# A kernel that plans its own order of work gets other prices for its instructions

## The chip, the cores and the metric

The kernel runs on one core of one Trainium2 chip. The metric is the device time of one execution in microseconds (us). The core has five instruction queues that work in order and wait for each other by semaphores: TensorE (PE, with its weight loads as PEld), VectorE (DVE), ScalarE (ACT), GpSimd (POOL) and SyncE (SP), which issues every DMA here.

## The reference

The program is a two-layer backbone over 1024 latent tokens and, in the first layer, 256 context tokens, 1024 channels wide, in float32. What a layer computes:

```
h = modulate(rms_norm(x, norm1_g[l]), sh1, sc1)        # sh, sc, g from a conditioning vector
p = h @ w_in[l]                                        # columns of four head groups
y_a = fourier_mix(p[..., 0:256])                       # 2-D FFT, real part
y_b = neighbourhood_attention(q, k, v, k_ctx, v_ctx, rpb, rows)     # 8x16 windows, and the context
y_c = spatial_gating(p[..., 1024:1536], ...)           # gelu, layer norm, matmul over chunks of 128
y_d = diff_post(diff_latent(q, k, v, ...))             # (softmax(s1) - lam * softmax(s2)) @ v, rope
x = x + g1 * (concat(y_a, y_b, y_c, y_d) @ w_out[l])
h2 = modulate(rms_norm(x, norm2_g[l]), sh2, sc2)
x = x + g2 * (square(relu(h2 @ w_ff1[l])) @ w_ff2[l])
```

The context tokens go the same way in the first layer; a final RMSNorm ends it.

## The kernel before, in words

Channels lie on the 128 partitions and tokens along the free axis, in blocks of 512, 512 and 256 (BLK). To keep precision, each float32 operand is split into a high and a low part that TensorE takes in its fast format (F32R), and a product is three matmuls (`mm3`, L394). ACT makes the high part, DVE or POOL subtracts it to get the low one (`split`, L358).

By time, layer 0 has its projections and attention until about 900 us and its MLP until about 1700; layer 1 has projections and attention until about 2400, then a last MLP in seven products in place of eight (`mlp_last`, L1488), and the final norm.

The text of the kernel doesn't fix the order of the instructions. Every call of an engine goes to the class `Plan`, whose `add` (L131) records it with the earlier instructions that it depends on, the tiles that it uses, a rank and a price (`cost`, L160). At the end `flush` (L186) plays a list schedule: of the five engines it takes the one that can start first (L250 to L261); among the instructions of that engine that are ready by then it takes the one of lowest rank, then the first recorded (L262 to L265); it lets the engine be busy for the price, and lets those that depend on it become ready at the end of it plus `LAT`, 0.13 us (L274; from matmul to matmul without it). A DMA keeps SP for 0.06 us, the transfers follow one another at 320 KB a us, and data lands a fixed latency later (L267 to L270). Tiles have few buffers, so an instruction can also wait for the release of one. The order found is then issued as it is (L286), and each engine keeps to it. That is why nearly every instruction in the profile has the line L286; tiles are told apart by name.

The ranks come from `run(rank, erank, ...)` (L576): `rank` is for PE, `erank` for the other engines. In a layer, differential attention has rank 1 (L1952). Behind it on PE, at rank 2, stand Fourier, gating and the projections of neighbourhood attention (L1951), whose other engines have 0.5, ahead of attention; then neighbourhood attention at 3 (L1953), then the first part of the output projection at 4 (L1957). They fill PE's time while attention isn't ready.

A unit of differential attention (`unit`, L1040) writes scores (tile ds) into three PSUM banks, takes the maximum with DVE (mx, nm), the exponential with its sum with ACT (e), joins the two softmaxes on DVE, or on DVE and POOL. Then PE transposes (tp), ACT and DVE split the result (pt), and PE multiplies it with the values (pvd). Neighbourhood attention does the same with nsl and nsc, npt and pvn.

Other names: dks and dqs are keys and queries reloaded, wh, wl and w weights, nvw the values of neighbourhood attention written in 16 windows at a time (`put_nv`, L947), fr the squared relu of the first MLP, fy, fyh and fyl the Fourier result, its high and its low part.

Of the kernel before, what the change touches and what calls it, by code (L numbers as in the profile page):

```python
# [11 lines left out]
F32R = mybir.dt.float32r  # L12
# [4 lines left out]
PSUM = bass.MemoryType.PSUM  # L17
# [16 lines left out]
class Plan:  # L34
# [8 lines left out]
    def __init__(self, tc):  # L43
        self.tc, self.nc = tc, tc.nc
        self.rank = self.erank = 0.0
        self.ops = []
        self.done = 0
        self.hist = {}
        self.tiles = {}
        self.tags = {}  # L50
        self.masks = {}
        self.free = {}
        self.idle = []
        self.dma_free = 0.0


    def pool(self, pool):
# [102 lines left out]
    def cost(self, eng, method, outs, ins, kw):  # L160
        def width(a):
            n = 1
            for _, k in a.ap[1:]:
                n *= k
            return n

        n = max(width(a) for a in outs + ins)
        if eng == "tensor":
            n = width(outs[0])
            c = 1 if ins[0].dtype == F32R else 2 if method == "transpose" else 4  # L170
            return max(n, 128 if c == 4 else 64) * c / 2400.0
        if eng == "sync":
            b = 4
            for _, k in outs[0].ap:
                b *= k
            return b
        if eng == "scalar":
            return 0.093 + n / 1200.0 + (0.13 if kw.get("accum_out") is not None else 0.0)
        if eng == "vector":
            ptr = any(isinstance(kw.get(k), bass.AP) for k in ("scalar", "scalar1", "scalar2"))  # L180
            fast = method in ("tensor_scalar", "tensor_copy", "memset") and all(a.space != PSUM for a in outs + ins)
            return 0.065 + 0.065 * ptr + n / (1920.0 if fast else 960.0)
        return 0.1 + n / 470.0


    def flush(self):  # L186
        ops, base = self.ops, self.done
        n = len(ops)
        left, succ, ready = {}, {}, {}
        tiles, tags = self.tiles, self.tags  # L190
        waiting = {}
        engines = ("tensor", "vector", "scalar", "gpsimd", "sync")
        future = {e: [] for e in engines}
        avail = {e: [] for e in engines}

        def allocate(key):
            q = tags[key]
            while q[2] < q[0] and q[1]:
                t = q[1].pop(0)
                q[2] += 1  # L200
                tiles[t][2] = q[3]
                for i in waiting.pop(t, ()):
                    settle(i, q[3])

        def settle(i, t):
            ready[i] = max(ready[i], t)
            left[i] -= 1
            if left[i] == 0:
                heapq.heappush(future[ops[i][0]], (ready[i], i))

        pend = {}
        for i in range(base, n):
            for t in ops[i][5]:
                pend[t] = pend.get(t, 0) + 1

        def release(t):
            q = tags[tiles[t][0]]
            if q[1]:
                q[2] -= 1
                q[3] = max(q[3], tiles[t][3])  # L220
                allocate(tiles[t][0])
            else:
                self.idle.append(t)

        idle, self.idle = self.idle, []
        for t in idle:
            if t not in pend:
                release(t)
        for key in tags:
            allocate(key)  # L230
        for i in range(base, n):
            o = ops[i]
            left[i] = 1
            ready[i] = 0.0
            for j in o[4]:
                if j >= base:
                    left[i] += 1
                    succ.setdefault(j, []).append(i)
                else:
                    ready[i] = max(ready[i], ops[j][8])  # L240
            for t in o[5]:
                if tiles[t][2] is None:
                    left[i] += 1
                    waiting.setdefault(t, []).append(i)
                else:
                    ready[i] = max(ready[i], tiles[t][2])
            settle(i, 0.0)
        order = []
        while len(order) < n - base:
            best = None  # L250
            for e in engines:
                f = self.free.get(e, 0.0)
                if avail[e]:
                    s = f
                elif future[e]:
                    s = max(f, future[e][0][0])
                else:
                    continue
                if best is None or s < best[0]:
                    best = (s, e)  # L260
            s, e = best  # L261
            while future[e] and future[e][0][0] <= s:  # L262
                _, i = heapq.heappop(future[e])
                heapq.heappush(avail[e], (ops[i][6], i))
            _, i = heapq.heappop(avail[e])  # L265
            o = ops[i]
            if e == "sync":  # L267
                self.free[e] = s + 0.06
                self.dma_free = max(self.dma_free, s) + max(0.3, o[7] / 320e3)
                end = self.dma_free + 1.9  # L270
            else:
                end = s + o[7]
                self.free[e] = end
            o[8] = end + self.LAT  # L274
            order.append(i)
            for k in succ.get(i, ()):
                settle(k, end if e == "tensor" and ops[k][0] == "tensor" else o[8])
            for t in o[5]:
                pend[t] -= 1
                tl = tiles[t]  # L280
                tl[3] = max(tl[3], o[8])
                if pend[t] == 0:
                    release(t)
        for i in order:
            o = ops[i]
            ins = o[1](*o[2], **o[3])  # L286
            self.tc.keep_in_program_order(ins)
            o[1] = o[2] = o[3] = None
        self.done = n
# [1863 lines left out]
```

## Time and profile before

| what | us |
|---|---|
| median of 3 runs (lowest, highest) | 3067.13 (3064.72, 3068.18) |
| the profiled execution, its own time | 3063.9 |
| its span, first to last instruction | 3062.1 |
| PE busy | 2860.1 |
| DVE busy | 2036.7 |
| ACT busy | 1370.6 |
| POOL busy | 735.9 |
| mean granted clock of PE | 0.972 |

The busy time of an engine is the time in which at least one of its instructions ran. Instructions of one engine can overlap at their ends, so the spacing of two starts can be shorter than a duration. A wait in the profile is idle time of an engine just before an instruction, put down to whatever ended it.

### The profile page before, as it was taken

The page shows a single profiled execution, that of the slowest core. Times are in us where ns is not written, and L with a number is a line of the kernel's source. Part 1 is how long each engine was busy: PE and PEld are TensorE (multiplying, and loading weights), DVE is VectorE, ACT ScalarE, POOL GpSimd, SP SyncE. Part 2 cuts the span into 40 slices and gives each one's busy share as a digit, 9 for nine tenths or more (in the row PEclk, how much of TensorE's full clock was granted, in tenths as well). Part 3 has the DMA queues.
Part 4 walks back from the last instruction along what each step waited for, and adds up shares of the span by engine and source line. Part 5 has one row for each costly group of instructions (what it writes and reads, how often), then busy time and mean ns, then how long its engine had stood idle before and what let it go on. Part 6 is the DMA issues. An engine that isn't in the chain of part 4 may idle for free. (4 is left out here: it accounts for less than half of the span.)

```text
span 3062.1 us, 42936 instructions
## 1 busy us (share of the span) xinstructions
PE 2860.1 (93%) x14994; PEld 2352.7 (77%) x14994; DVE 2036.7 (67%) x3753; ACT 1370.6 (45%) x2974; POOL 735.9 (24%) x507
## 2 busy tenths in 40 slices
PE   6898999999999999999999888898998999999997
PEld 3776787776788888888888777777786778878876
DVE  7477886586866677665333647786785875576765
ACT  5466555475423233222122436655564544454332
POOL 5235222243522122112112303311110022122200
PEclk8898999999999999999999999999999999999998
DMA  6644345677347886674211364445688664464465
GB/s 229 193 131 135 104 125 154 238 248 254 97 138 246 285 277 216 221 239 137 65 39 45 131 194 128 148 155 167 215 281 305 226 211 145 145 219 149 150 228 177
DMA packets 291632, 550.60 MB, mean 180 GB/s; under 512 B 35924, under 2 KB 84692, under 8 KB 288344
## 3 DMA queue, kind: packets, MB, share of 16 engines
q1 hardware_dynamic: 291416, 547.86, 54.4%
q8 instruction: 118, 1.93, 0.3%
q14 instruction: 98, 0.80, 0.1%
HBM read 388.58 MB, written 162.88 MB: 180 GB/s over the span
## 5 line engine op out<-in xcount | busy, mean ns | idle before, releaser
L286 POOL TENSOR_TENSOR wl<-wr,wh 128x512 fp32r<-128x512 f32 (+2 forms) x260 | 360.5, 1408 | 919.8 <-ACT wh L286 894.6
L286 PE MATMUL sx<-bq,sh 128*128 128x512 f32 x2304 | 548.4, 396 | 10.3 <-ACT q L286 3.2
L286 PEld LDWEIGHTS sx<-bq,sh 128*128 128x128 f32 x2304 | 431.1, 188 | 121.3 <-DVE bq L286 6.5
L286 DVE TENSOR_REDUCE mx<-ds 128x1 f32<-128x512 f32 (+1 forms) x320 | 218.4, 686 | 131.8 <-PE ds L286 129.9
L286 ACT ACTIVATE e<-ds,nm 128x512 f32<-128x512 f32 (+1 forms) x400 | 241.3, 611 | 121.2 <-DVE nm L286 111.3
L286 ACT ACTIVATE wh<-wr 128x512 fp32r<-128x512 f32 (+2 forms) x260 | 152.5, 614 | 316.9 <-issue 139.4
L286 PE MATMUL f<-hidh,wh 128*128 128x512 f32 (+1 forms) x768 | 278.1, 362 | 6.9 <-ACT hh L286 4.1
L286 PE MATMUL f<-hidl,wh 128*128 128x512 f32 (+1 forms) x768 | 277.0, 361 | 0.0
L286 PE MATMUL f<-hidh,wl 128*128 128x512 f32 (+1 forms) x768 | 277.0, 361 | 0.0
L286 PE MATMUL f<-hh,wh 128*128 128x512 f32 (+1 forms) x768 | 274.5, 357 | 0.0
L286 PE MATMUL f<-hh,wl 128*128 128x512 f32 (+1 forms) x768 | 274.2, 357 | 0.0
L286 PE MATMUL f<-hl,wh 128*128 128x512 f32 (+1 forms) x768 | 274.2, 357 | 0.0
L286 PE MATMUL pj<-hh,wh 128*128 128x512 f32 (+1 forms) x512 | 194.8, 381 | 21.2 <-DMA wh<-wd 9.4
L286 DVE SCALAR_TENSOR_TENSOR x<-f,ada,x 128x512 f32<-128x512 f32 (+1 forms) x192 | 125.5, 658 | 130.8 <-PE f L286 130.5
L286 PE MATMUL pj<-hl,wh 128*128 128x512 f32 (+1 forms) x512 | 193.4, 378 | 2.3 <-POOL hl L286 1.9
L286 PE MATMUL pj<-hh,wl 128*128 128x512 f32 (+1 forms) x512 | 193.0, 377 | 0.5 <-DMA wl<-wd 0.5
L286 ACT ACTIVATE sh<-wq 128x512 fp32r<-128x512 f32 x160 | 99.2, 628 | 202.0 <-DMA wd<-sh 49.1
L286 POOL TENSOR_TENSOR e<-e 128x1280 f32<-128x1280 f32 (+1 forms) x36 | 98.4, 2733 | 378.5 <-DVE e L286 239.1
L286 POOL TENSOR_TENSOR ws<-wq 128x512 f32<-128x512 f32 x54 | 76.8, 1422 | 416.6 <-DVE sh L286 233.6
L286 DVE TENSOR_TENSOR fr<-fr 128x512 f32<-128x512 f32 (+1 forms) x96 | 84.7, 882 | 133.7 <-ACT fr L286 133.5
L286 PE MATMUL ds<-dks,dqs 128*128 128x512 f32 (+1 forms) x400 | 143.0, 393 | 32.2 <-ACT e L286 18.8
L286 PEld LDWEIGHTS f<-hidh,wh 128*128 128x128 f32 x768 | 146.5, 191 | 31.1 <-ACT hh L286 4.5
(315 smaller groups left out, 6577.4 us busy)
## 6 DMA issues: line engine op xcount, KB each, us to landing
wd<-sh SPq DMA_DIRECT2D x99, 512.0 KB, 3.9
wr<-in_w_ff SPq DMA_DIRECT2D x144, 256.0 KB, 3.1
ar<-in_ada_w SPq DMA_DIRECT2D x112, 256.0 KB, 3.7
bq<-hid SPq DMA_DIRECT2D x24, 1024.0 KB, 6.8
wq<-in_w_ff1s SPq DMA_DIRECT2D x76, 256.0 KB, 3.1
sh<-wd SPq DMA_DIRECT2D x66, 256.0 KB, 4.2
wq<-in_w_ff2s SPq DMA_DIRECT2D x64, 256.0 KB, 4.2
wr<-in_ada_w SPq DMA_DIRECT2D x48, 256.0 KB, 3.8
```

Of the source, the lines that this page charges most:

```text
L286: ins = o[1](*o[2], **o[3])
```

## The change: other prices in the planner, and a port that two engines share

`cost` gets other formulas for every engine: durations with a fixed part and a part by elements, those of ACT depending on whether an operand is in PSUM. A new function `shares` tells which instructions use the SBUF port that DVE and POOL have in common: all of POOL, and of DVE those with two inputs in SBUF, and copies and scalar operations on SBUF. In `flush` such an instruction starts no earlier than the end of the last one that used the port. The latency of a DMA behind its transfer becomes 2.6 us. Ranks, `LAT`, SP's 0.06 us and the instructions themselves stay.

```diff
--- before.py
+++ after.py
@@ -52,6 +52,7 @@
         self.free = {}
         self.idle = []
         self.dma_free = 0.0
+        self.port = 0.0
 
 
     def pool(self, pool):
@@ -167,20 +168,35 @@
         n = max(width(a) for a in outs + ins)
         if eng == "tensor":
             n = width(outs[0])
-            c = 1 if ins[0].dtype == F32R else 2 if method == "transpose" else 4
-            return max(n, 128 if c == 4 else 64) * c / 2400.0
+            if ins[0].dtype == F32R:
+                return max(0.112, 0.006 + n / 2265.0)
+            if method == "transpose":
+                return 0.107
+            return max(0.224, n / 600.0)
         if eng == "sync":
             b = 4
             for _, k in outs[0].ap:
                 b *= k
             return b
+        near = any(a.space == PSUM for a in ins)
         if eng == "scalar":
-            return 0.093 + n / 1200.0 + (0.13 if kw.get("accum_out") is not None else 0.0)
+            return (0.165 if near else 0.195) + n / 1200.0 + (0.21 if kw.get("accum_out") is not None else 0.0)
         if eng == "vector":
             ptr = any(isinstance(kw.get(k), bass.AP) for k in ("scalar", "scalar1", "scalar2"))
             fast = method in ("tensor_scalar", "tensor_copy", "memset") and all(a.space != PSUM for a in outs + ins)
-            return 0.065 + 0.065 * ptr + n / (1920.0 if fast else 960.0)
-        return 0.1 + n / 470.0
+            return 0.15 + 0.06 * ptr + n / (1920.0 if fast else 960.0)
+        return 0.2 + n / 465.0
+
+    def shares(self, o):
+
+        if o[0] == "gpsimd":
+            return True
+        if o[0] != "vector":
+            return False
+        ins = [v for k, v in o[3].items() if k in ("in_", "in0", "in1") and isinstance(v, bass.AP)]
+        if any(a.space == PSUM for a in ins):
+            return False
+        return len(ins) > 1 or o[9] in ("tensor_scalar", "tensor_copy")
 
 
     def flush(self):
@@ -267,8 +283,11 @@
             if e == "sync":
                 self.free[e] = s + 0.06
                 self.dma_free = max(self.dma_free, s) + max(0.3, o[7] / 320e3)
-                end = self.dma_free + 1.9
+                end = self.dma_free + 2.6
             else:
+                if self.shares(o):
+                    s = max(s, self.port)
+                    self.port = s + o[7]
                 end = s + o[7]
                 self.free[e] = end
             o[8] = end + self.LAT
```

## Rows read from the trace of the kernel before

**Rows 1.** Busy line of the page: engine, busy us, share of the span, instructions.

```profile
PE 2860.1 (93%) x14994; PEld 2352.7 (77%) x14994; DVE 2036.7 (67%) x3753; ACT 1370.6 (45%) x2974; POOL 735.9 (24%) x507
```

**Rows 2.** Table by stage: stretch, us, busy us of PE, PEld, DVE, ACT, POOL; clock; DMA.

```profile
0.00:100.00 100.00, 66.84 (x277) 46.16 (x278) 72.93 (x131) 53.32 (x89) 48.22 (x36) 0.85 0.65 226
100.00:900.00 800.00, 736.53 (x4252) 596.92 (x4251) 561.15 (x1238) 438.65 (x1114) 268.72 (x196) 0.97 0.52 162
900.00:1700.00 800.00, 798.25 (x4155) 676.96 (x4154) 452.44 (x636) 210.49 (x381) 162.10 (x114) 1.00 0.53 176
1700.00:2500.00 800.00, 718.61 (x4005) 600.09 (x4004) 584.14 (x1240) 424.00 (x1022) 157.90 (x90) 0.96 0.62 200
2500.00:3000.00 500.00, 496.01 (x2118) 396.73 (x2118) 330.18 (x440) 231.15 (x350) 91.49 (x66) 1.00 0.51 176
3000.00:3062.00 62.00, 43.85 (x195) 35.84 (x193) 35.90 (x69) 12.98 (x20) 7.44 (x6) 0.83 0.47 160
```

**Rows 3.** Waits of PE: tile, what ended them, us in total, times, longest us.

```profile
PE ds L286 <- ACT e L286: 18.8, 25, 2.7
...
PE ds L286 <- DMA dks<-dk: 9.7, 3, 4.8
PE pj L286 <- DMA wh<-wd: 9.4, 2, 6.9
...
PE wo L286 <- DMA w<-wd: 5.9, 6, 3.6
...
PE tp L286 <- DVE e L286: 4.9, 6, 1.5
...
PE pvn L286 <- DVE npt L286: 3.1, 7, 0.7
...
PE pvd L286 <- DVE pt L286: 2.6, 8, 0.6
```

**Rows 4.** DVE in groups of one shape: out<-in, count, busy us, mean ns, idle before.

```profile
L286 DVE TENSOR_REDUCE mx<-ds 128x1 f32<-128x512 f32 x256 | 175.3, 687 | 131.1 <-PE ds L286 129.4
...
L286 DVE TENSOR_TENSOR pt<-tp,pt 128x512 fp32r<-128x512 f32 x168 | 111.4, 684 | 30.1 <-ACT pt L286 28.9
...
L286 DVE SCALAR_TENSOR_TENSOR e<-e,dr 128x1280 f32<-128x1280 f32 x32 | 52.8, 1650 | 0.6
...
L286 DVE TENSOR_TENSOR fr<-fr 128x256 f32<-128x256 f32 x32 | 40.5, 1265 | 17.8 <-ACT fr L286 17.8
...
L286 DVE TENSOR_SCALAR e<-e,dr 128x1280 f32<-128x1280 f32 x32 | 29.4, 918 | 0.9
```

**Rows 5.** Timeline of 1951 to 1963 us: start, us, instruction, idle before and its end.

```profile
1951.48 0.16 DVE L286 TENSOR_REDUCE nm<-mx 128x1 f32<-128x3 f32 x1
...
1951.67 0.69 ACT L286 ACTIVATE e<-ds,nm 128x512 f32<-128x512 f32 x1 [0.53 <-DVE nm L286]
...
1952.35 0.68 ACT L286 ACTIVATE e<-ds,nm 128x512 f32<-128x512 f32 x1
...
1955.23 0.68 DVE L286 TENSOR_TENSOR fy<-fT,fT 128x512 f32<-128x512 f32 x1
...
1955.94 0.63 ACT L286 ACTIVATE fyh<-fy 128x512 fp32r<-128x512 f32 x1 [2.36 <-DVE fy L286]
...
1960.31 1.28 DVE L286 TENSOR_TENSOR pt<-tp,pt 128x512 fp32r<-128x512 f32 x2
```

**Rows 6.** Timeline of 2088 to 2102 us, SP's queue and then PE.

```profile
2088.18 7.59 SPq L286 DMA_DIRECT2D nvw<-vt  x16
...
2101.86 0.80 PE L286 MATMUL pj<-hh,wh 128*128 128x512 f32 x1 [6.93 <-DMA wh<-wd]
```

**Rows 7.** Table as rows 2, of a stretch after a wait and one without idle.

```profile
2095.00:2107.00 12.00, 5.14 (x15) 4.09 (x16) 1.71 (x5) 2.25 (x7) 1.71 (x1) 0.57 0.78 238
...
2500.00:2600.00 100.00, 100.00 (x430) 80.55 (x430) 61.65 (x92) 50.30 (x82) 20.86 (x16) 1.00 0.46 156
```

**Rows 8.** DMA issues: count, KB each, median us from issue to landing.

```profile
dks<-dk SPq DMA_DIRECT2D x32, 320.0 KB, 4.9
```

## The prediction, made before the changed kernel ran

> **What bounds the kernel now.** I read the busy line of the page first: TensorE (PE) is busy 2860.1 of 3062.1 us [rows 1], so 202.0 us of the span it is idle, and no order of the same instructions can take much more than that. Then the table by stage [rows 2]: the two MLP stages leave it next to nothing (800 - 798.2 and 500 - 496.0, 5.7 us in all), the start holds 33.2 and the end 18.2 us in single chains with nothing beside them, and the two stages with attention hold 63.5 and 81.4, together 144.9 us. That is where an order of work can be better or worse. The list of PE's waits [rows 3] tells what ends them: many short waits on ScalarE (ACT) and VectorE (DVE), 25 of them on the exponentials alone (18.8 us), and few long ones on DMA (9.7, 9.4 and 5.9 us, 11 waits, 25.0 us). So the kernel is bound by PE, and it loses 4.7% of its span in the two attention stages to engines that stand in the planned order while what they need isn't there yet.
>
> **What the change is, in prices.** No instruction and no wait is added or removed. The planner gets other prices, and out of them another order on all five queues. I worked out each price before and after for the commonest shape, and set them beside the trace.
>
> PE, 512 columns: 0.213 before, 0.006 + 512/2265 = 0.232 after. In a stretch without idle time 430 matmuls took 100 us, 0.2326 each [rows 7]. The new price is right, the old 8% low.
>
> DVE, 512 elements: 0.065 + 512/960 = 0.598 before, 0.683 after. An instruction of this kind, pt, lasts 0.684 [rows 4], so the new price is its duration. But two of them take 1.28 together [rows 5], so the second starts 1.28 - 0.684 = 0.60 after the first: the engine is taken for 0.60, the old price. From the start of one to the start of what waits for it: 1955.94 - 1955.23 = 0.71 [rows 5]; the planner's end plus its 0.13 gave 0.728 before and gives 0.813 now. For a three-element maximum 1951.67 - 1951.48 = 0.19; before 0.198, now 0.283. The change prices the tail of each DVE instruction twice.
>
> ACT, an exponential of 512 elements with its row sum: 0.650 before, 0.802 after. In the trace one starts 0.68 after the one before it (1952.35 - 1951.67) [rows 5]. A copy out of PSUM goes from 0.520 to 0.592. So ACT was near the trace and is now 14 to 23% dearer.
>
> DMA: the latency behind the transfer goes from 1.9 to 2.6 us. For the 320 KB key loads the plan said 1.02 + 1.9 + 0.13 = 3.1 us and says 3.8 now; the trace has a median of 4.9 [rows 8]. Here the change goes the right way, by 0.70 us a load, and not far enough.
>
> Shared port: a DVE instruction with two SBUF inputs can't start in the plan while GpSimd (POOL) works. The trace has such a block: fr on 256 elements lasts 1265 ns on average [rows 4], where 0.15 + 256/960 = 0.417 is its price alone. So the rule is real. POOL's own price goes up by 9%.
>
> So four prices move toward the trace (PE, DMA, port, POOL) and two, DVE and ACT, away from it. What counts for an order is the ratio: PE 9% dearer, DVE 14%, ACT 14 to 23%: against PE the other two get 5 to 13% slower in the plan.
>
> **The sum.** (a) Loads. A plan that expects a load 0.70 later puts other PE work before its consumer. Bounds: nothing, and 11 x 0.70 = 7.7 us off the DMA waits of rows 3. The longest of them isn't of that kind: at 2094.9 PE stands 6.93 us because SP issues 16 small writes of nvw in 7.59 us ahead of the weights [rows 6], 0.47 us each, where the plan's 0.06 for an issue isn't touched. I take half, 4 us.
> (b) Links. Between a score matmul and the exponential that frees its bank lie a reduction, a maximum and an exponential: 0.085 + 0.085 + 0.152 = 0.32 us dearer. PE's own work in between, about 2 us, gets 9% dearer too, 0.18, so the plan puts some 0.14 us more of other work before the next score matmul. 25 waits by 0.14 is 3.5 us (at most 25 x 0.32 = 8.0, at least nothing). For transposes and value matmuls the link is one ACT and one DVE instruction, 0.157 dearer; 6 + 7 + 8 = 21 waits in rows 3, at most 3.3 us, and after PE's own share half of it, 1.5. Together 5 us.
> (c) Port. The longest overlaps are in fr, in the first MLP, where PE is busy 798.2 of 800 us [rows 2], so its 32 late instructions cost nothing now and save nothing. Elsewhere the planner still starts the POOL instruction as soon as it can; it knows of the block but doesn't avoid it. I take 0, within 5 us either way.
> (d) Clock. Behind the 6.93 us wait the granted clock of 2095 to 2107 was 0.57, partly at the lower level of 1.2 GHz, and PE was busy 5.14 us there [rows 7]; 0.43 x 5.14 = 2.2 us lost on top of 6.9. So a long wait costs another third. A third of (a) and (b) is 3 us.
> What the reordering costs elsewhere I can't see in rows; it is in the rivals. Sum: 4 + 5 + 0 + 3 = 12 us. The profiled execution took 3063.9 us (span 3062.1 and 1.8 around it): 3051.9. The median of the runs shown, 3067.1, is 3.2 us above it, so the forecast is 3055. With the upper ends, (7.7 + 8.0 + 3.3 + 5) x 1.33 = 32, it would be 3035; with the lower ends, 0, 0 and -5 by 1.33, 7 us slower than before.
>
> **Rivals.**
> Filler spent too early, slower. PE's projections, Fourier and gating matmuls have a lower priority than the differential attention and fill its pauses. With DVE and ACT priced 14% dear the plan sees longer pauses, gives PE more filler for each step of attention, and runs out of it with attention still to do. The chain of attention is then alone. Its DVE work, two layers, is 175.3 + 111.4 + 52.8 + 29.4 = 368.9 us [rows 4] for 488 instructions, 328 us at the spacing; the PE work beside these is 256 x 0.233 for scores, 672 transposes at the 0.107 that both plans have, and 672 value matmuls of half 0.233, 210 us in all. So PE would idle 36% of such a stretch. 14% of 328 is 46 us more of it, 16.5 us of idle time, 22 with the clock's third: 3063.9 + 22 + 3.2 = 3089. By the net 5% it is 8 us. It decides when the end of an attention stage (the last 200 us before the output projection) idles by more than 7 us above now. For it: DVE and ACT really are mispriced. Against it: neighbourhood attention and the output projection's head stand behind as more filler.
> For this rival speaks the Trainium skill, page Perfetto Trace Analysis, section Optimizing Scalar/DVE Operations: profiled durations of these engines hold a write-acknowledgement that overlaps the next instruction, and the engine itself is kept by a smaller fixed cost, about 60 ns for DVE on SBUF. By that page's figure a 512-element DVE instruction keeps its engine 0.593 us, against the 0.60 of rows 5: the trace agrees, and the duration is the wrong number to plan an engine's time with. (For DVE on PSUM the page has 125 ns, 0.658; the spacing of pt, read from PSUM, is 0.60, so there the trace decides.)
> The order hardly matters: same. Ratios move by 5 to 13%, the two attention stages are held by their dependencies and buffers, and the idle time moves without shrinking: 3061 to 3073.
> More is gained than I count. 120 of the 144.9 us aren't on DMA; were a third of them misplaced order that longer links cure, 40 us and 13 of clock go: 3063.9 - 53 + 3.2 = 3014. Against it: nearly all of rows 3 are short waits in a chain, and they don't show whether other work was ready.
>
> **How the numbers follow.** The forecast, faster by some 12 us, gets 0.36, with 3037 to 3060 for itself; the larger gain 0.12; no change (within 0.2%, 6 us, about what a measurement can tell) 0.20; filler spent too early, or another place where the new order runs dry, 0.32. Faster is 0.36 + 0.12 = 0.48. The range leaves out half of the larger gain (0.06) below 3018, and above 3097 the worst third of the slower case (0.1).
>
> **What would show it.** Right: PE's idle time in 100 to 900 and in 1700 to 2500 falls from 144.9 to about 135 us, waits on exponentials from 18.8 to about 15, DMA waits of PE by about 4, and the MLP stages keep their length. The 7 us stall behind the writes of nvw stays, if these still stand ahead of the weights. Wrong: PE's idle time in the attention stages grows, and at their ends; then the doubled tails of DVE and ACT are the cause. A changed length of an MLP stage would contradict all of it.

## The result: slower by 2.2%, and the profile after

| what | before, us | after, us |
|---|---|---|
| median of the runs compared (4 and 4) | 3067.65 | 3136.79 |
| ratio, 95% interval | 1 | 1.0221 [1.0203, 1.024] |
| the profiled execution, its span | 3063.9, 3062.1 | 3141.44, 3139.6 |
| PE busy | 2860.1 | 2898.9 |
| PE idle (span less busy) | 202.0 | 240.7 |
| granted clock | 0.972 | 0.960 |

The forecast was 3055 us, the range 3018 to 3097; the time lies above it. Of the 77.5 us that the span grew, PE is idle for 38.7 and busy for 38.8 more, with the same 14994 matmuls. Most of the second half is the clock. Over the whole span, idle time included, 3062.1 x 0.028 = 86 us weren't granted before and 3139.6 x 0.040 = 126 are not now; over PE's busy time alone, worked out from the trace's records of the granted clock, it is 65 and 96, so some 31 of the 38.8. No run here shows where the other 8 come from.

The busy line and the table by stage, as [rows 1] and [rows 2]:

```profile
PE 2898.9 (92%) x14994; PEld 2376.0 (76%) x14994; DVE 2026.6 (65%) x3753; ACT 1375.5 (44%) x2974; POOL 736.3 (23%) x507
```

```profile
0.00:100.00 100.00, 64.31 (x289) 42.69 (x289) 75.45 (x137) 55.25 (x93) 47.12 (x36) 0.90 0.73 245
100.00:900.00 800.00, 727.60 (x4087) 584.85 (x4088) 544.83 (x1211) 432.58 (x1097) 260.32 (x192) 0.94 0.50 155
900.00:1700.00 800.00, 797.82 (x4174) 677.28 (x4174) 454.68 (x647) 208.31 (x377) 158.21 (x112) 1.00 0.54 179
1700.00:2500.00 800.00, 699.95 (x3860) 584.37 (x3859) 527.72 (x1163) 397.56 (x978) 148.83 (x82) 0.94 0.58 183
2500.00:3000.00 500.00, 489.32 (x2073) 390.51 (x2072) 337.35 (x463) 240.47 (x375) 113.11 (x78) 0.99 0.48 164
```

PE idles 72.4 and 100.0 us in the two stretches with attention (100 to 900 and 1700 to 2500), 172.4 where it was 144.9. The stages have moved against these limits, so I also measured them by their own marks: the first and last matmul of the first MLP (f), and the first matmul of the last MLP (sx). Rows of the kernel after for these tiles: form, count, duration in ns (least, median, most), first and last start, shapes.

```profile
L305 PE MATMUL f<-hh,wh x768: 276/393/792, 846.9 to 1716.4; 128*128 128x512 f32 x128, 128*128 128x256 f32 x64
...
L305 PE MATMUL f<-hidh,wl x768: 276/393/632, 912.5 to 1782.9; 128*128 128x512 f32 x128, 128*128 128x256 f32 x64
...
L305 PE MATMUL sx<-bq,sh x2304: 388/394/792, 2464.9 to 3115.1; 128*128 128x512 f32 x192
```

And of the kernel before:

```profile
L286 PE MATMUL f<-hh,wh x768: 276/393/482, 825.1 to 1691.1; 128*128 128x512 f32 x128, 128*128 128x256 f32 x64
...
L286 PE MATMUL f<-hidh,wl x768: 276/393/632, 883.6 to 1770.3; 128*128 128x512 f32 x128, 128*128 128x256 f32 x64
...
L286 PE MATMUL sx<-bq,sh x2304: 388/394/504, 2393.6 to 3037.6; 128*128 128x512 f32 x192
```

Up to the first f it takes 846.9 in place of 825.1 (+21.8); the first MLP 936.0 in place of 945.2 (-9.2); from its end to the first sx, which is layer 1's attention, 682.0 in place of 623.3 (+58.7); the rest 674.7 in place of 668.5 (+6.2). So the loss stands in the two attention stages, most of it in the second.

**What happens there.** Three kinds of PE work can fill the pauses of differential attention, and are called filler here: the projections pj and their like, then neighbourhood attention (nsl), then the head of the output projection (wo). The same view, for layer 0 (100 to 900 us), of the kernel before:

```profile
L286 PE MATMUL pj<-hh,wl x267: 276/393/628, 100.7 to 572.2; 128*128 128x512 f32 x86, 128*128 128x256 f32 x48
...
L286 PE MATMUL ds<-dks,dqs x208: 274/392/775, 132.5 to 568.1; 128*128 128x512 f32 x64, 128*128 128x256 f32 x40
...
L286 PE MATMUL nsl<-nsa x64: 337/342/522, 575.2 to 702.7; 128*128 128x384 f32 x64
```

And after:

```profile
L305 PE MATMUL pj<-hh,wl x264: 276/393/628, 101.1 to 535.5; 128*128 128x512 f32 x85, 128*128 128x256 f32 x47
...
L305 PE MATMUL ds<-dks,dqs x208: 277/394/797, 125.1 to 604.4; 128*128 128x512 f32 x64, 128*128 128x256 f32 x40
...
L305 PE MATMUL nsl<-nsa x64: 338/423/686, 610.0 to 737.3; 128*128 128x384 f32 x64
```

Before, the projections end 4 us behind the last score matmul. After, they end 37 us earlier and the scores 36 us later, so for 69 us differential attention runs without them. In layer 1 the scores outlast the projections by 25 us before (2183.5, 2208.4) and by 87 after (2195.2, 2282.1). In these two stretches of the kernel after PE is hardly idle (4.8 of 69 us and 10.6 of 87): it takes wo. Busy time of wo alone, in stretches of 50 us, before and then after (stretch, us, busy us and count; the last three numbers are the granted clock, the DMA share and GB/s of the stretch):

```profile
550.00:600.00 50.00, 4.00 (x13) 0.97 0.83 288
600.00:650.00 50.00, 21.10 (x62) 0.93 0.71 231
650.00:700.00 50.00, 12.87 (x42) 1.00 0.78 255
700.00:750.00 50.00, 25.65 (x108) 1.00 0.85 295
...
2250.00:2300.00 50.00, 17.96 (x58) 1.00 0.89 302
2300.00:2350.00 50.00, 26.95 (x89) 0.93 0.89 310
```

```profile
550.00:600.00 50.00, 17.57 (x62) 0.93 0.55 187
600.00:650.00 50.00, 12.76 (x45) 0.93 0.59 199
650.00:700.00 50.00, 0.00 (x0) 0.90 0.61 203
700.00:750.00 50.00, 6.46 (x16) 0.90 0.59 181
...
2300.00:2350.00 50.00, 0.00 (x0) 0.86 0.61 207
2350.00:2400.00 50.00, 3.23 (x8) 0.97 0.61 180
```

So the last filler is spent beside differential attention, and neighbourhood attention, which it used to accompany, stands almost alone. From the last score matmul ds to the last nsl, in layers 0 and 1 (columns as in [rows 2]), before and then after:

```profile
568.10:702.70 134.60, 124.97 (x731) 97.86 (x730) 104.22 (x273) 87.70 (x249) 52.62 (x46) 0.96 0.81 273
2208.40:2314.00 105.60, 99.27 (x614) 86.08 (x614) 86.04 (x234) 70.54 (x201) 14.63 (x7) 0.98 0.80 265
...
604.40:737.30 132.90, 106.92 (x611) 85.57 (x610) 104.86 (x267) 86.76 (x246) 50.01 (x44) 0.91 0.59 190
2282.10:2390.30 108.20, 85.53 (x529) 71.92 (x527) 83.98 (x232) 73.14 (x207) 15.54 (x8) 0.94 0.65 203
```

PE idles 9.6 and 6.3 us in them before, 26.0 and 22.7 after: 32.8 us more, most of the 38.7. All of PE's work in the stretches of 50 us of the kernel after:

```profile
650.00:700.00 50.00, 39.59 (x239) 0.90 0.61 203
700.00:750.00 50.00, 39.10 (x231) 0.90 0.59 181
...
2300.00:2350.00 50.00, 36.69 (x224) 0.86 0.61 207
2350.00:2400.00 50.00, 39.42 (x250) 0.97 0.61 180
```

There PE idles 10 to 13 us of 50, and the granted clock is down to 0.86 to 0.90 in three of the four and 0.97 in the last: part of these stretches ran at 1.2 in place of 2.4 GHz. PE's waits after, as [rows 3]:

```profile
PE tp L305 <- POOL e L305: 17.4, 15, 3.5
PE ds L305 <- ACT e L305: 16.8, 21, 2.2
...
PE nsl L305 <- ACT e L305: 6.8, 8, 1.6
PE wo L305 <- DMA y<-yd: 6.7, 4, 2.7
PE wo L305 <- DMA w<-wd: 6.6, 4, 5.0
PE pvd L305 <- DVE pt L305: 6.1, 7, 1.2
...
PE pj L305 <- DMA wh<-wd: 3.7, 3, 2.5
...
PE ds L305 <- DMA dks<-dk: 2.0, 2, 1.5
```

The waits that the prediction wanted shorter are shorter: on dks 2.0 in place of 9.7 us, of pj on wh 3.7 in place of 9.4, on exponentials 16.8 in place of 18.8. Others came in their stead. Transposes (tp) wait 17.4 us for POOL's part of attention, 0.2 before, and scores of neighbourhood attention (nsl) 6.8 us for ACT, again 0.2 before; of these 24.2 us 15.1 fall into the two stretches above. And all of PE's waits that a DMA ended come to 34.9 us before and 34.8 after: those for y and yh, and others, took the place of those for dks and wh.

### The profile page after: what moved, and what is told of

It is laid out like the page before. It is cut to its first block, busy times and chain, and to the rows that moved or that the text cites. A ratio compares the mean times of both kernels' runs of the same rounds, so it can differ in the third digit from the quotient of the medians.

```text
span 3139.6 us, 42893 instructions
## 1 busy us (share of the span) xinstructions
PE 2898.9 (92%) x14994; PEld 2376.0 (76%) x14994; DVE 2026.6 (65%) x3753; ACT 1375.5 (44%) x2974; POOL 736.3 (23%) x507
## 5 line engine op out<-in xcount | busy, mean ns | idle before, releaser
L305 PE MATMUL tp<-ident,e 128*128 128x128 f32 x992 | 167.8, 287 | 24.3 <-POOL e L305 17.4
```

## The experiments

The theories. **A**: filler is spent too early, because of the dearer DVE and ACT. **B**: the shared port does it. **C**: the ranks were tuned to the old prices, so any other prices lose. **D**: wrong DVE and ACT prices make bad orders anywhere, and exact ones would make a better order. A, B and C stood before the first four runs. After these D was added and A was widened to **A2**, a balance: the order is best when filler and attention run out together; dear DVE and ACT spend the filler early, dear PE and DMA leave some over.

All ratios are to the kernel before. "Scores outlast" is the last start of ds less that of the last projection or gating matmul, in layers 0 and 1, worked out from the trace as above; a negative number means that filler was left over.

| kernel | ratio, 95% interval | scores outlast, us |
|---|---|---|
| before | 1 | -4, 25 |
| after | 1.0221 [1.0203, 1.024] | 69, 87 |
| before with the DVE and ACT prices | 1.0407 [1.0384, 1.0429] | 116, 113 |
| ... the DVE price alone | 1.0312 [1.0294, 1.033] | 69, 87 |
| ... the ACT price alone | 1.014 [1.0118, 1.0161] | 26, 44 |
| ... the PE prices | 1.0247 [1.0226, 1.0269] | -45, -19 |
| ... the DMA latency | 1.0141 [1.0125, 1.0157] | -32, 15 |
| ... the port | 1.0059 [1.0039, 1.0079] | 25, 33 |
| ... prices at random within 1%, two seeds | 1.0023 [1.0012, 1.0034], 1.0013 [1.0001, 1.0025] | -12, 17; -2, 27 |
| ... a dearer DMA issue | 0.9981 [0.9971, 0.9991] | -4, 30 |
| after with the old DVE and ACT prices | 1.0025 [1.0013, 1.0038] | -31, -1 |
| ... a quarter of their rise | 1.0036 [1.0023, 1.005] | 9, 15 |
| ... no port | 1.0239 [1.0222, 1.0255] | 56, 71 |
| ... LAT 0.045 | 1.0291 [1.0272, 1.0309] | 59, 88 |
| ... engine time by spacing, LAT 0.045 | 1.0073 [1.0056, 1.009] | -22, 14 |
| ... engine time by spacing | 0.9989 [0.9979, 0.9999] | 2, 33 |
| ... PE 1.2 times as dear | 1.0136 [1.0116, 1.0156] | 7, 19 |
| ... filler behind attention | 1.0471 [1.0456, 1.0487] | -81, -53 |
| ... part of the filler behind attention | 1.0265 [1.0242, 1.0288] | -27, -1 |

The second column gives a direction and no more. The kernel after and the DVE price alone both stand at 69 and 87 and lose 2.21 and 3.12%; the DMA latency alone and the kernel after with the old prices stand near each other in layer 0 (-32, -31) and lose 1.41 and 0.25%.

**Each part of the change alone, in the kernel before.** The DVE and ACT prices:

```diff
-            return 0.093 + n / 1200.0 + (0.13 if ...)
+            return (0.165 if near else 0.195) + n / 1200.0 + (0.21 if ...)
-            return 0.065 + 0.065 * ptr + ...
+            return 0.15 + 0.06 * ptr + ...
```

> The kernel before with only the new DVE and ACT prices. In its PE order 56 of 208 and 58 of 192 score matmuls stand behind the last filler matmul (before: 0 and 14; the whole change: 36 and 50). Theory A (filler spent too early, through the DVE and ACT prices): the slowest of the four, 1.5 to 4% above before, since more scores are left alone than in the whole change, whose loss is 2.2%. Theory B (the shared port delays POOL and what waits for it): within 0.5% of before. Theory C (the ranks were tuned to the old prices, any other price loses): 1 to 2.5% slower, like the other three.

It loses 4.07%, more than the whole change. Its scores and projections in layer 0:

```profile
L287 PE MATMUL pj<-hh,wl x272: 276/393/628, 103.5 to 540.9; 128*128 128x512 f32 x87, 128*128 128x256 f32 x49
...
L287 PE MATMUL ds<-dks,dqs x208: 274/394/796, 136.0 to 657.0; 128*128 128x512 f32 x64, 128*128 128x256 f32 x40
```

116 us without projections. These two prices are enough for the loss, and the others take some of it back.

The port (`shares` and the three lines in `flush`, no price):

> The kernel before with only the shared port in the plan. 16 and 20 scores stand behind the last filler. Theory A: a small loss, 0 to 0.8%. Theory B: most of the change's loss, 1.2 to 2.2%, with transposes waiting 15 us or more for POOL's sums. Theory C: 1 to 2.5%.

0.59%: a real cost when alone, a quarter of the loss, so B doesn't carry it.

The DMA latency (1.9 to 2.6):

> The kernel before with only the DMA latency of 2.6 us in the plan. 0 and 8 scores stand behind the last filler, about as before. Theory A: within 0.5% of before, with somewhat less PE idle time on DMA. Theory B: the same as before. Theory C: 1 to 2.5% slower.

1.41% slower, with projections left over behind the last scores in layer 0. A, which had it within 0.5%, missed; C had the size. One long wait is new:

```profile
PE ada L286 <- DMA wr<-in_ada_w: 10.2, 2, 9.1
```

And PE's waits on exponentials are 29.7 us, 18.8 before. What in the order brings them isn't shown.

The PE prices:

> The kernel before with only the new PE prices. No score stands behind the last filler; 176 and 61 filler matmuls stand behind the last score. Theory A: not slower than before, -1 to +0.3%, since filler is left where attention ends. Theory B: the same as before. Theory C: 1 to 2.5% slower.

2.47% slower, in the other direction: the projections end 45 us behind the scores in layer 0. The first MLP gets longer as well, since PE now waits for DVE in it, where the kernel before had 2.8 us in 3 waits of this kind:

```profile
PE f L289 <- DVE x L289: 14.0, 12, 2.3
```

So right PE prices alone lose as much as the change, and A as first told (only DVE and ACT do harm) is too narrow: hence A2. C had this size too, and missed those of the port and of the DVE and ACT prices.

**Parts taken back in the kernel after.** The old DVE and ACT formulas:

> The changed kernel with the old DVE and ACT prices back; PE, POOL and DMA prices and the port stay. In its PE order no score stands behind the last filler; 114 filler matmuls in layer 0 and 7 in layer 1 stand behind the last score. Theory A2 (balance: the kernel is fastest when filler and differential attention run out together; each price pushes the meeting point one way, DVE, ACT and port to filler spent early, PE and DMA to filler left over): like the kernel with the DMA latency alone, which had 118 filler matmuls left over, 0.8 to 1.6% slower than before. Theory D (the doubled DVE and ACT tails alone are what is wrong): as fast as before or faster, -1 to +0.3%. Theory C (any price other than the tuned ones loses, whatever the balance): 1 to 2.5% slower.

Of the 2.2% no more than 0.25% is left. The PE, DMA, port and POOL prices together cost 8 us; the rest is the two prices. D had this, A2 didn't (0.8 to 1.6%).

A quarter of their rise:

```diff
-            return (0.165 if near else 0.195) + ... (0.21 if ...)
+            return (0.093 + 0.25 * (0.072 if near else 0.102)) + ... (0.1500 if ...)
-            return 0.15 + 0.06 * ptr + ...
+            return 0.08625 + 0.0625 * ptr + ...
```

> The changed kernel with a quarter of the rise in the fixed part of DVE and ACT. All other prices, the port and the DMA latency are those of the change, so the order is new everywhere, but it is balanced: 6 and 8 scores stand behind the last filler and no filler behind the last score (before: 0 and 14, with 27 filler matmuls left over in layer 0). Theory A2: within 0.5% of before, some 1.5 to 2.5% faster than the change. Theory C: 1 to 2.5% slower than before. Theory D: between the change and the kernel with the old DVE and ACT prices.

0.36%: not better than none of it, and scores outlast projections by 9 and 15 us.

DVE and ACT keep their engines only for the spacing of rows 5, and results follow 0.045 behind the whole duration:

```diff
-    LAT = 0.13
+    LAT = 0.045
-                self.free[e] = end
+                self.free[e] = end - (0.085 if e == "vector" else 0.1 if e == "scalar" else 0.0)
```

> The changed kernel, but DVE and ACT are busy in the plan only for their spacing (duration less 0.085 and 0.1 us), and LAT is 0.045, so that results come when the trace shows them. It is the most exact planner here. 70 filler matmuls are left over in layer 0, 8 scores alone in layer 1. Theory A2: 0.2 to 1% slower than before. Theory D (exact prices make a better order): 0.5 to 1.5% faster than before. Theory C: 1 to 2.5% slower.

0.73% slower. For DVE and ACT these are the prices nearest to the trace of all that were run, so the second half of D falls: nearer to the trace wasn't faster. Two thirds of the loss is gone all the same.

Filler's other engines behind attention (`run(r + 2, r + 0.5, ...)` to `r + 1.5`), in the kernel after:

> The changed kernel with the non-PE work of the filler ranked behind differential attention (1.5 in place of 0.5). 314 and 216 filler matmuls are left over when the last score is done. Theory A2: far over on the other side, 3 to 6% slower than before, slower than the change, with neighbourhood attention starting later than in it. If filler spent early were the only harm (theory A of the first runs): faster than the change, within 1% of before.

4.71% slower: the filler is starved and 314 and 216 of its matmuls are left over. The wrong side is as dear as the other, as A2 said.

**Balance by rank, chance, and the port taken out.** Gating and the projections of neighbourhood attention alone get the later rank:

> The changed kernel with all of its prices; only the last two pieces of the filler (gating and the projections of neighbourhood attention) get rank 1.5 in place of 0.5 on the engines other than PE, behind differential attention. 100 filler matmuls in layer 0 and 5 in layer 1 are left over when the last score is done, no score stands behind the last filler (the change: 36 and 50 scores alone). Theory A2 (the meeting point of filler and attention decides, prices act through it): 0.2 to 1% slower than before, so half or more of the change's 2.2% is back with none of its prices undone. Theory D (the dear DVE and ACT prices make bad orders everywhere): still 1.8 to 2.5% slower.

A2 missed here: scores and projections end within 27 us and 1 us of each other, and it is still 2.65% slower. Its longest waits:

```profile
PE ds L305 <- ACT e L305: 38.5, 33, 6.0
```

PE waits 38.5 us for exponentials where it waited 18.8 before. The later rank puts the ACT and DVE work of that filler behind attention's, so its matmuls may not be ready when attention pauses; this reason is argued, not shown. Ends that meet are no proof of a good order in between.

Each price of the kernel before times a random number within 1%, two seeds:

> The kernel before with each price of an engine changed at random by up to 1% either way: a new order without a new model. 47 filler matmuls left over in layer 0, 11 scores alone in layer 1. Theory A2: within 0.7% of before. Theory C (any price other than the tuned ones loses): 1 to 2.5% slower.

> As the run before with another seed: 17 filler matmuls left over in layer 0, 17 scores alone in layer 1. Theory A2: within 0.5% of before. Theory C: 1 to 2.5% slower. The two runs together tell how far a time moves by a new order alone.

0.23 and 0.13% slower, so the order before is a little better than a chance one near it, and C, in the form that any other price loses some per cent, falls. That the ranks suit the old set of prices isn't ruled out by it: each of the five larger changes made alone (DVE, ACT, PE, DMA, port) lost 0.6 to 3.1%. It also says what size of difference one order may have by luck: some 0.2%.

No port, in the kernel after:

> The changed kernel without the shared port. 30 and 38 scores stand behind the last filler (the change: 36 and 50). Theory A2: 0.3 to 0.8% faster than the change, 1.4 to 1.9% slower than before. If the port caused most of the loss (theory B): within 0.7% of before.

2.39%. Taking the port away wins nothing; B is out. A2 had 1.4 to 1.9%, since fewer scores are left alone: a miss.

**The ratio, and what the tail does.** All PE prices of the kernel after times 1.2, which is wrong by itself but brings the ratio to DVE and ACT back near the old one:

> The changed kernel with PE's prices raised by 20%: now PE is mispriced like DVE and ACT. 6 and 12 scores stand behind the last filler, none of it is left over (the change: 36 and 50 scores alone). Theory A2 (ratio and meeting point decide): at most 0.7% slower than before, 1.5 to 2.2% faster than the change, though one more price is wrong. Theory D (wrong prices make bad orders anywhere): 1.8 to 3.5% slower than before.

Some 40% of the loss goes, less than A2 said (at most 0.7% slower) and more than D did (1.8 at least). Layer 0 up to the first f takes 828.1 us, against 825.1 before and 846.9 after. The loss stands elsewhere: layer 1's attention takes 648.8 us, 623.3 before and 682.0 after, and the first MLP 959.7, 945.2 before, where PE waits as with the PE prices alone:

```profile
PE f L305 <- DVE x L305: 13.7, 11, 2.6
```

So in layer 0's attention the ratio decides, not the single price; over the whole kernel one factor can't mend it. PE's idle time is 199.3 us in this version, no more than before: its loss is all in longer busy time (2907.5 us), of which the clock, counted as above, explains less than half.

The DVE and the ACT price each alone, in the kernel before:

> The kernel before with the new DVE prices alone. 40 and 48 scores behind the last filler, about as many as in the change. Theory A2: 1.8 to 2.8% slower than before. Theory D: somewhere between 0.3 and 4%, without a tie to the number of scores.

> The kernel before with the new ACT prices alone. 16 and 26 scores behind the last filler, 42 together, little more than with the port alone (36, 0.6% slower). Theory A2: 0.5 to 1.3% slower than before. Theory D: no tie to the scores.

3.12 and 1.40%, together 4.5 where both at once cost 4.07: nearly a sum, and DVE has two thirds of it. Both lie a little above what A2 had.

LAT 0.045 in place of 0.13 in the kernel after, so that the end of the duration and what follows it are as in the trace:

> The changed kernel with LAT 0.045 in place of 0.13, so a result of DVE or ACT is due when the trace shows it; the engines are still busy for the whole duration. 34 and 47 scores behind the last filler. Theory A2, with the harm in the time on the engine: 1.6 to 2.5% slower than before, about as the change. If the lateness of results does the harm: 0.2 to 0.9% slower.

2.91%: it doesn't help to have the results earlier in the plan, it costs 0.7% more (A2 had 2.5 at most). That late results do the harm is out.

The engine's time by the spacing again, but with LAT left at 0.13:

> The kernel after, in which an instruction of VectorE or ScalarE keeps its engine 0.085 or 0.1 us less than its price, while what depends on it still becomes ready at the whole price plus 0.13 us. So results are as late in the plan as in the kernel after, and only the engine's time goes back. Theory A2 (the time charged on the engine does the harm, because it makes the plan spend other matmuls too early): the last score matmuls of the two layers again stand with at most 20 matmuls of their kind behind the last filler, and the kernel is 0.2 to 0.9% slower than before, near the 0.73% of the version with the lateness taken out as well. Rival (the late results do the harm): it stays near the 2.2% of the kernel after, 1.8 to 2.6%.

0.11% faster than before (the interval ends just under 1). Results are here as late in the plan as in the kernel after, and only the engine's time went back: that alone takes away the whole loss, and more of it than A2 said. Its rows for layer 0:

```profile
L305 PE MATMUL pj<-hh,wl x265: 276/393/501, 100.2 to 556.1; 128*128 128x512 f32 x85, 128*128 128x256 f32 x48
...
L305 PE MATMUL ds<-dks,dqs x208: 274/394/795, 126.9 to 558.5; 128*128 128x512 f32 x64, 128*128 128x256 f32 x40
```

Both end together again, as before, and both 10 to 16 us earlier. Its stretches with attention:

```profile
100.00:900.00 800.00, 742.61 (x4292) 600.44 (x4291) 562.83 (x1243) 438.16 (x1115) 265.40 (x197) 0.97 0.52 162
...
1700.00:2500.00 800.00, 717.64 (x3986) 598.98 (x3985) 579.36 (x1237) 420.35 (x1019) 159.72 (x89) 0.95 0.61 198
```

57.4 + 82.4 = 139.8 us idle, 144.9 before and 172.4 after. From the last score to the last nsl it is 12.2 and 9.0 us, 26.0 and 22.7 in the kernel after.

The issue of a DMA at 0.45 us on SP in place of 0.06, in the kernel before:

> The kernel before, with one price changed: an issue of a DMA keeps SP 0.45 us in the plan in place of 0.06. In the trace of the kernel before 16 small writes take SP 7.59 us, 0.47 each, and TensorE stands 6.93 us for the weights behind them. The plan of this version leaves 27 filler matmuls over in layer 0 and runs 18 score matmuls short in layer 1, as the plan before (27 and 14). If a price that is wrong on the path of a wait is worth mending: the 6.93 us wait goes or shrinks to under 3 us and the kernel is 0.1 to 0.3% faster than before. Rival (any other order than the one at hand loses, and SP's queue is dear in no other place): within 0.2%, or 0.1 to 0.3% slower, as with prices moved at random by 1%.

0.19% faster, the fastest of all. The long wait behind the writes of nvw is halved, from 6.9 to 3.2 us, a little over what I had set. The waits of this kind together:

```profile
PE pj L286 <- DMA wh<-wd: 7.6, 3, 3.6
```

Both faster versions gain no more than the random prices lost, so that their gain comes from the righter price and not from luck isn't shown. The two together weren't run.

## Why the prediction was wrong, step by step

**What bounds the kernel, and which prices are off**: this held. The loss is in the attention stages, and the step "The change prices the tail of each DVE instruction twice" names the cause that the runs found: taking the tail off the engine's time alone turned 2.21% slower into 0.11% faster. Of the two times it is the engine's that did the harm: with the tail taken out of LAT in its stead the loss was 2.91%.

**(b) Links** is the step that failed. It said that dearer links make the plan put "some 0.14 us more of other work before the next score matmul", and booked that as a gain of 5 us, while the cost of it stood in the sum at nothing ("What the reordering costs elsewhere I can't see in rows; it is in the rivals"). The waits on exponentials did shrink, from 18.8 to 16.8 us; those of tp, pvn and pvd on DVE, 10.6 us in [rows 3], grew to 12.4 (1.2, 5.1 and 6.1), so the gain was 0.2. And the other work comes out of a fixed stock; what is put in early is missing at the end, where PE idled 32.8 us more between the last ds and the last nsl of the two layers.

**The rival "filler spent too early"** had the mechanism and the sign, at a chance of 0.32 and a price of 22 us; it cost 69. Three things in it were mis-sized. First, it took 14% of 328 us as 46 us more of attention alone; measured by the ends of scores and projections it is 73 us in layer 0 and 62 in layer 1, 135. I had counted 488 instructions of 512 elements. The tail is a fixed 0.085 us per instruction, and a three-element maximum goes from 0.068 to 0.153; the stretches of [rows 2] with attention hold 1238 + 1240 DVE instructions, 2478 x 0.085 = 211 us more of planned DVE time (an estimate, since not all of these are attention's), and ACT's come on top. Second, the argument against it, that neighbourhood attention and wo "stand behind as more filler", was turned round: wo was taken early, and neighbourhood attention then stood alone, 10 to 13 us idle in 50. Third, the clock.

**(d) Clock**: "a long wait costs another third" came from one long wait. Here 38.7 us of idle time went with 38.8 of longer busy time. That the two are equal is chance: with the DVE price alone they are 54.1 and 38.3, with the PE prices alone 26.8 and 49.2. The prediction took PE's busy time as fixed but for the clock, and it isn't: it moves with the order. Putting 135 us and this factor into the rival's own working (36% of 135, times 2, less the gain of 12) gives 85, near the 69 measured, but by luck: in those 135 us PE was hardly idle, since wo filled them, and the idle time came behind them.

**(a) Loads**: I took 4 us. The three DMA waits of [rows 3] went from 25.0 to 2.0 + 3.7 + 6.6 = 12.3, but others came (6.7 of wo on y, 4.3 on yh, 3.4 of pv on wh, 3.4 of ada on its weights), and PE's DMA waits as a whole stayed at 34.9 and 34.8: the term was 0. What the longer latency does in it isn't shown: alone it lost 1.41%.

**(c) Port**: 0 within the change, as said (2.21% with it, 2.39% without). Alone it costs 18 us, outside my bound of 5.

**What would show it**: the growth of idle time at the ends was named as the sign of the wrong case, with the doubled tails as its cause, and that is what came. "A changed length of an MLP stage would contradict all of it" was wrong: it got 9 us shorter here, 19 us longer with the PE prices and 7 us shorter with the port alone, which changes no price. What sets its length isn't shown.

**Open**: why the PE prices alone lose 2.47% and the DMA latency 1.41%, while both with the port and POOL's price lose only 0.25%. The balance gives the direction of each, not the size of the sum. Open too is why with the results later in the plan (LAT 0.13) the exact engine times are 0.8% faster than with the exact 0.045, and what beside the clock makes PE's busy time longer in some orders.

## What to carry to other kernels

In a plan, an engine's time and a result's time are two numbers: charge the engine the spacing of back-to-back instructions and give the duration to what depends on it. Here that alone took away two thirds of the loss with results due when the trace shows them, and all of it with results 0.085 us later. Before prices are changed in a list schedule with filler, add up what the change does to each engine's planned total, small instructions included, and ask which filler runs out first and what then stands alone; a shorter wait now is paid for from that stock. Prices that are right one at a time can lose when others stay wrong: change them together, and measure.

## What the runs showed of the hardware

Many short pauses cost TensorE its clock too. From the last score to the last nsl PE idled 9.6 of 134.6 us in layer 0 before, at a granted clock of 0.96, and 26.0 of 132.9 after, at 0.91; in layer 1 it was 6.3 of 105.6 at 0.98 and 22.7 of 108.2 at 0.94. For the same 14994 matmuls PE was busy 38.8 us longer, some 31 of them by the clock. The one long wait of [rows 6] and [rows 7] had let me expect a third of the idle time.

The clock isn't all. With the engine's time by spacing and LAT 0.045, PE idled 3.8 us less than before, at a granted clock of 0.970 against 0.972, and was busy 25.3 us longer (2885.4) with the same matmuls. So the order moves PE's busy time by itself; no run here shows how.
